# Delta rule: the off-diagonal blocks of the inverses in one group of matmuls a head, the first head's half of them amid its first gate projection

## The chip, the cores and the metric

The kernel runs on one core of one Trainium2 chip. The metric is the device time of one execution in microseconds (us), the median of several runs. Beside the timed runs there is one execution under the hardware profiler; all rows of the profile come from it, and times inside it are counted from the start of its span.

## The reference

The reference is one layer of a hybrid decoder for a prompt of 1024 tokens with 16 learned tokens ahead of it and a sample group of 8 sequences of 8 tokens: a half-step feed-forward network, a mixer, and a second half-step network. The mixer projects the tokens once and runs two branches, a gated delta rule with 8 heads and a sliding-window attention. What matters here is the delta rule for the prompt. In each chunk it solves a unit lower triangular system (cut):

```python
a_mat = jnp.where(strict, beta[..., :, None] * kk * decay, 0.0) + jnp.eye(c, dtype=q.dtype)
sol = lax.linalg.triangular_solve(a_mat, rhs, left_side=True, lower=True, unit_diagonal=True)
...
u = u_b - jnp.einsum('nhcd,nhde->nhce', w_c, s)
o = jnp.einsum('nhcd,nhde->nhce', qd_c, s) + jnp.einsum('nhij,nhje->nhie', qk_c, u)
s = s * cd_c[..., None, None] + jnp.einsum('nhcd,nhce->nhde', kd_c, u)
```

The reference uses chunks of 64 tokens. The kernel uses chunks of 128, eight a head, and holds the transposed inverse of each chunk's matrix as a tile of 128 x 128. Such an inverse has two diagonal blocks of 64 x 64, the inverses of the halves, and one off-diagonal block, the product of one half's inverse, the block of the matrix between the halves, and the other half's inverse.

## The kernel before, in words

The kernel goes through the layer in stages: first network, keys of all heads, window attention, the heads of the delta rule, output projection, second network. The change is in the stage of the heads (`heads`, L1664), between 1272 and about 1837 us of the profiled execution.

TensorE's order is written by hand: `body` puts it under a manual schedule (L1889), so TensorE executes matmuls exactly in the order in which the program's text issues them. The order of every other engine, and of the loads on the sync queue (SP), is set by a planner, which simulates the program while it is built; single instructions can be pinned to the order of the text. Waits between engines follow from the tiles that an instruction reads and writes. A tile with one buffer cannot be filled again before its last reader is done.

Streams of work are generators, and `weave` (L145) interleaves them. Each stream has a start, an end and a number of steps; step i of n stands at start + (end - start) (i + 0.5) / n, and the steps of all streams are issued in the order of these positions.

For each head h the streams are:

- `chain(h)`, 29 steps: the recurrence over the sample and eight chunks. Chunk t multiplies by the inverse in L1615, `R[:, i, :]` of the tile for t // 4.
- `qv_steps` and `z_gate`: projections, long runs of matmuls into the tile "gu" (L128, L130, L132), three for each of 8 slices of the model's width, in pieces of 512, 256 and 320 or 336 columns. They fill TensorE between the steps of the others.
- `prep8(h)`: three steps of preparation for the sample group (L1503 for "kq", L1541, L1550); its loads are "kq", "dt8" and "kd8".
- `prep(h, g)`: preparation of four chunks, g = 0 for chunks 0 to 3 and g = 1 for chunks 4 to 7. It has five steps, and each takes a turn of the PSUM tile "tr", one bank with one buffer: the off-diagonal first products (L1466, copied to "xt" by ScalarE in L1468), the values' transposes (L1474, scaled by ScalarE in L1476), the off-diagonal second products (L1480, copied into R in L1482), the squares of the queries (L1503, L1505), and keys by queries (L1491, finished by VectorE in L1493). Its first step also issues all loads of the group: the diagonal blocks into R (two, L1454), the transposed inverses "rt" (L1455), the matrix blocks "bo" (L1456), then kf, pm and kd; and GpSimd clears the lower left block of R (L1451).

The first and second products are matmuls of 64 x 64 at tile positions (0, 64) and (64, 0) of the array: the first reads partitions 0 to 63 and writes 64 to 127, the second the other way.

`prep(h, 1)` runs in the first 35% of head h. `prep8(h + 1)` and `prep(h + 1, 0)` run as `early(h + 1)`, eight steps, in the last quarter of head h (the last fifth of head 0). For head 0 there is a separate beginning, `early0` (L1669): its eight steps stand in the last 30% of the first 72 matmuls of head 0's gate projection z0. Its order is the off-diagonal first products, one step of `prep8`, nine small loads of the sample's inverses (`solves8`, "r8", L1430 and L1431), the other four steps of `prep`, and the last two of `prep8`.

Of the kernel before, what the change touches and what calls it, by code (L numbers as in the profile page):

```python
# [18 lines left out]
P = 128  # L19
# [120 lines left out]
def drain(steps):  # L140
    for _ in steps:
        pass


def weave(*streams):  # L145

    order = sorted((a + (b - a) * (i + 0.5) / n, j) for j, (g, a, b, n) in enumerate(streams) for i in range(n))
    for _, j in order:
        next(streams[j][0], None)
    for g, *_ in streams:  # L150
        drain(g)
# [7 lines left out]
def steps_of(g, n):  # L159

    return itertools.islice(g, n)
# [493 lines left out]
H = 8  # L655
# [43 lines left out]
class Mixer:  # L699
# [733 lines left out]
    def persistent(self, pool):  # L1433
        c, nc = self.c, self.nc
        self.ms = [c.t(pool, [P, 8, P], tag=f"ms{i}") for i in range(1)]
        self.p8 = [c.t(pool, [80, P], tag=f"p8{i}") for i in range(2)]
        self.on8 = c.t(pool, [P, 1, P], tag="on8")
        for m in (*self.ms, *self.p8, self.on8):
            nc.gpsimd.memset(m, 0.0)

    def prep(self, h, g, pool):

        c, nc = self.c, self.nc
        T = lambda shape, tag, bufs=None, dt=F32: c.t(pool, shape, dt, tag=tag, bufs=bufs)
        x = self.hd[h]
        ts = range(4 * g, 4 * g + 4)
        cols = slice(4 * g * P, (4 * g + 4) * P)
        R = x["R", g] = T([P, 4, P], f"R{g}")
        rt = T([64, 4, 64], "rt", 2)
        bo = T([64, 4, 64], "bo", 2)  # L1450
        nc.gpsimd.memset(R[64:P, :, 0:64], 0.0)  # L1451
        for half in range(2):
            r = slice(half * 64, half * 64 + 64)
            nc.sync.dma_start(R[r, :, r], self.lr_d[h, ts.start:ts.stop, half].rearrange("t r c -> r t c"))  # L1454
        nc.sync.dma_start(rt, self.lrt_d[h, ts.start:ts.stop, 0].rearrange("t r c -> r t c"))  # L1455
        nc.sync.dma_start(bo, self.bo_d[h][:, ts.start:ts.stop])  # L1456
        kf = x["kf", g] = T([P, 4, P], f"kf{g}")
        nc.sync.dma_start(kf, self.kf_d[h][:, cols].rearrange("p (t k) -> p t k", k=P))
        pm = x["pm", g] = T([P, 4, P], f"pm{g}")
        nc.sync.dma_start(pm, self.dt_d[h][:, ts.start:ts.stop, :])  # L1460
        kd = x["kd", g] = T([P, 4, P], f"kd{g}")
        nc.sync.dma_start(kd, self.kd_d[h][:, ts.start:ts.stop, :])

        px = self.ps([P, 4, P], "tr")
        for t in range(4):
            nc.tensor.matmul(px[64:P, t, 0:64], bo[:, t, :], rt[:, t, :], start=True, stop=True, tile_position=(0, 64))  # L1466
        xt = T([P, 4, 64], "xt")
        nc.scalar.copy(xt[64:P], px[64:P, :, 0:64])  # L1468
        yield

        vs = x["vs", g] = T([P, 4, P], f"vs{g}")
        pt = self.ps([P, 4, P], "tr")
        for i, t in enumerate(ts):
            nc.tensor.transpose(pt[:, i, :], x["cv"][:, t * P:(t + 1) * P], self.k(C_IDENT))  # L1474
        for i, t in enumerate(ts):
            nc.scalar.activation(vs[:, i, :], pt[:, i, :], AF.Copy, scale=self.nr[:, h, t:t + 1])  # L1476
        yield
        px = self.ps([P, 4, P], "tr")
        for t in range(4):
            nc.tensor.matmul(px[0:64, t, 0:64], xt[64:P, t, :], R[64:P, t, 64:P], start=True, stop=True,  # L1480
                             tile_position=(64, 0))
        nc.scalar.copy(R[0:64, :, 64:P], px[0:64, :, 0:64])  # L1482
        yield

        cq = x["cq", g] = T([P, 4], f"cq{g}")
        self.squares(h, cq, [x["qv"][:, t * P:(t + 1) * P] for t in ts], pool)
        yield

        pk = self.ps([P, 4, P], "tr")
        for i, t in enumerate(ts):  # L1490
            nc.tensor.matmul(pk[:, i, :], kf[:, i, :], x["qv"][:, t * P:(t + 1) * P], start=True, stop=True)  # L1491
        for i, t in enumerate(ts):
            nc.vector.scalar_tensor_tensor(out=pm[:, i, :], in0=pk[:, i, :], scalar=self.s[:, h, t:t + 1],  # L1493
                                           in1=pm[:, i, :], op0=ALU.mult, op1=ALU.mult)
        yield
# [58 lines left out]
    def chain(self, h, pool):  # L1554
# [44 lines left out]
        for t in range(8):  # L1599
            if t % 4 == 0:  # L1600
                on = T([P, 4, P], "on", 3)
                vs, kf, R, kd, pm = (x[k, t // 4] for k in ("vs", "kf", "R", "kd", "pm"))
            i = t % 4
# [10 lines left out]
            px = self.ps([P, P], "ch", 2)  # L1614
            nc.tensor.matmul(px, R[:, i, :], b, start=True, stop=True)  # L1615
            xs = T([P, P], "xs", 2)
# [47 lines left out]
    def heads(self, pool, mg):  # L1664
        def early(h):
            yield from self.prep8(h, pool)
            yield from self.prep(h, 0, pool)

        def early0():  # L1669
            prep = self.prep(0, 0, pool)  # L1670
            yield from steps_of(prep, 1)
            yield from steps_of(prep8, 1)
            self.solves8(pool)
            yield from prep
            yield from prep8

        z0 = self.z_gate(0, pool)
        prep8 = self.prep8(0, pool)
        weave((steps_of(z0, 72), 0, 1, 72), (early0(), 0.7, 1, 8))
        for h in range(H):  # L1680
            streams = [(self.chain(h, pool), 0, 1, 29), (self.prep(h, 1, pool), 0, 0.35, 5)]
            if h:
                streams += [(self.emit(h - 1, pool), 0, 0.2, 3)]
            if h < H - 1:
                if h:
                    streams += [(self.qv_steps(h + 1, pool), 0, 0.5, 145), (self.z_gate(h, pool), 0.5, 1, 145)]
                else:
                    streams += [(self.qv_steps(1, pool), 0, 0.55, 145), (z0, 0.55, 1, 73)]
                streams += [(early(h + 1), 0.75 if h else 0.8, 1, 8)]
            else:  # L1690
                out = self.emit(h, pool)
                streams += [(self.z_gate(H - 1, pool, mg.load_w), 0, 0.95, 145), (steps_of(out, 2), 0.6, 1.15, 2)]
                begin = mg.begin()
                streams += [(steps_of(begin, 1), 0.6, 0.6, 1)]
            weave(*streams)
        weave((begin, 0, 1, 42), (out, 0.1, 0.2, 1), (self.left, 0.15, 0.5, 4))
        drain(mg.begin_last(self.hd[H - 1]["Z"][:, 0:P]))
# [496 lines left out]
```

## Time and profile before

| what | us |
|---|---|
| median of 3 runs | 2669.71 |
| lowest and highest run | 2668.64 and 2669.86 |
| the profiled execution's own time | 2674.25 |
| span of the profiled execution | 2672.4 |
| mean granted TensorE clock over the span | 0.99 |

In the rows, PE is TensorE's matmuls and PEld its weight loads, DVE is VectorE, ACT is ScalarE, POOL is GpSimd, SPq is the sync queue that issues loads. A row names the line, the engine, the operation, the tile written and the tiles read, the shape and the count. A matmul in full precision has two records. In a time-ordered row the first two numbers are the start and the length of the row's instructions taken together, and the brackets at the end say how long the engine sat idle before and who ended that. In a row of waits the three numbers are the total in us, the number of times, and the longest.

### The profile page before, as it was taken

Reading aid. Unit: us, or ns where it says so; the run is one execution under the profiler, and the core shown is the slowest. Engines: PE = TensorE matmul, PEld = TensorE weight load, DVE = VectorE, ACT = ScalarE, POOL = GpSimd, SP = SyncE. Lnnn points to the kernel's source line nnn. Section 1 sums busy time; section 2 is a strip of 40 time slices with the busy share of each in tenths; the row PEclk is TensorE's granted clock in tenths of the full one; section 3 lists DMA queues with packets and bytes.
Section 4 is the critical chain, followed back from the end, with each engine's and each line's share of the span. In section 5 each row is a group of like instructions: output and inputs, shape, how many; then the busy total and the mean of one; then the engine's idle time right before and its main releaser. Section 6 shows DMA issues by size and latency. Waiting matters only on the chain. (4 is left out here: it accounts for less than half of the span.)

```text
span 2672.4 us, 49500 instructions
## 1 busy us (share of the span) xinstructions
PE 2606.7 (98%) x19053; PEld 2486.6 (93%) x19053; DVE 1552.0 (58%) x2315; ACT 1127.5 (42%) x2718; POOL 1270.3 (48%) x1205
## 2 busy tenths in 40 slices
PE   7999999999999999999999999999999999999998
PEld 7999999999988998888889999997789999999998
DVE  7657565546677726995444444444556656654566
ACT  6333343422146734457444444454533434334221
POOL 6656555445525533433334333335555555554471
PEclk9999999999999999999999999999999999999999
DMA  4344343667545744345332233334433433338764
GB/s 165 122 150 155 122 167 117 248 230 250 190 141 165 222 140 130 114 135 158 102 99 89 87 97 96 100 93 159 163 107 139 164 128 149 127 138 318 241 226 142
DMA packets 229570, 406.47 MB, mean 152 GB/s; under 512 B 59751, under 2 KB 121351, under 8 KB 229047
## 3 DMA queue, kind: packets, MB, share of 16 engines
q1 hardware_dynamic: 209030, 324.75, 37.5%
q10 hardware_dynamic: 20304, 78.56, 7.4%
q8 instruction: 150, 2.46, 0.4%
q14 instruction: 86, 0.70, 0.1%
HBM read 264.36 MB, written 140.53 MB: 152 GB/s over the span
## 5 line engine op out<-in xcount | busy, mean ns | idle before, releaser
L132 PE MATMUL gu<-xh,wl 128*128 128x512 f32 (+3 forms) x1456 | 496.5, 341 | 0.0
L128 PE MATMUL gu<-xh,wh 128*128 128x512 f32 (+3 forms) x1456 | 492.3, 338 | 0.0
L130 PE MATMUL gu<-xl,wh 128*128 128x512 f32 (+3 forms) x1456 | 490.9, 337 | 0.0
L282 POOL TENSOR_TENSOR wl<-T,wh 128x512 fp32r<-128x512 f32 x246 | 331.2, 1353 | 319.2 <-ACT wh L281 251.7
L496 PE MATMUL y<-hb,wh 128*128 128x256 f32 (+2 forms) x2528 | 430.3, 290 | 3.3 <-DVE acc L507 1.8
L282 POOL TENSOR_TENSOR wl<-raw,wh 128x512 fp32r<-128x512 f32 x200 | 283.1, 1424 | 252.2 <-ACT wh L281 189.4
L496 PEld LDWEIGHTS y<-hb,wh 128*128 128x128 f32 x2528 | 365.9, 188 | 4.4 <-DVE acc L507 2.2
L281 ACT CAST wh<-T 128x512 fp32r<-128x512 f32 x246 | 152.5, 621 | 363.4 <-PE B L316 111.4
L132 PEld LDWEIGHTS gu<-xh,wl 128*128 128x128 f32 x1456 | 277.4, 191 | 16.6 <-issue 0.4
L128 PEld LDWEIGHTS gu<-xh,wh 128*128 128x128 f32 x1456 | 277.3, 190 | 16.7 <-issue 0.9
L130 PEld LDWEIGHTS gu<-xl,wh 128*128 128x128 f32 x1456 | 277.2, 190 | 16.6 <-issue 0.4
L496 PE MATMUL y<-hb,wl 128*128 128x256 f32 (+2 forms) x1264 | 271.6, 288 | 0.0
L281 ACT CAST wh<-raw 128x512 fp32r<-128x512 f32 x200 | 122.4, 621 | 279.4 <-PE C L316 82.9
L770 POOL TENSOR_TENSOR wl<-raw,wh 128x1024 fp32r<-128x1024 f32 x58 | 141.0, 2430 | 180.9 <-ACT wh L769 173.5
L507 DVE TENSOR_TENSOR acc<-acc,y 128x552 f32<-128x552 f32 (+4 forms) x216 | 144.7, 679 | 138.1 <-PE y L496 137.8
L496 PEld LDWEIGHTS y<-hb,wl 128*128 128x128 f32 x1264 | 206.9, 188 | 0.0
L256 DVE TENSOR_TENSOR T<-raw,raw 128x512 f32<-128x512 f32 x124 | 118.6, 961 | 108.0 <-POOL wl L282 108.0
L1570 POOL TENSOR_TENSOR f<-f,mhalf 128x1 f32<-128x1 f32 (+1 forms) x72 | 54.8, 761 | 126.2 <-DVE f L1568 124.6
L267 DVE TENSOR_TENSOR T<-raw,T 128x512 f32<-128x512 f32 x62 | 65.6, 1061 | 61.9 <-POOL wl L282 61.8
L256 DVE TENSOR_TENSOR T<-raw,T 128x512 f32<-128x512 f32 x62 | 62.1, 1010 | 32.0 <-POOL wl L282 31.6
L1075 DVE TENSOR_TENSOR ltmp<-la 72x14 f32<-72x14 f32 (+37 forms) x76 | 71.9, 946 | 12.6 <-DMA la<-b_d 11.6
L769 ACT CAST wh<-raw 128x1024 fp32r<-128x1024 f32 x60 | 63.0, 1050 | 38.1 <-PE gu L130 38.1
(593 smaller groups left out, 7312.5 us busy)
## 6 DMA issues: line engine op xcount, KB each, us to landing
hb<-hid SPq DMA_DIRECT2D x71, 552.0 KB
hb<-hid SPq DMA_DIRECT2D x71, 544.0 KB
hid<-hs ACTq DMA_DIRECT2D x69, 552.0 KB
hid<-hs ACTq DMA_DIRECT2D x69, 544.0 KB
raw<-in_w_in_dram SPq DMA_DIRECT2D x58, 512.0 KB
raw<-in_ffn_w_gate_dram SPq DMA_DIRECT2D x100, 256.0 KB
raw<-in_ffn_w_up_dram SPq DMA_DIRECT2D x94, 256.0 KB
raw<-in_ffn_w_down_dram SPq DMA_DIRECT2D x88, 256.0 KB
```

What stands on the lines that cost most here:

```text
L128: nc.tensor.matmul(ps, wh, xh, start=first and i == 0, stop=False)
L130: nc.tensor.matmul(ps, wh, xl, start=False, stop=False)
L132: nc.tensor.matmul(ps, wl, xh, start=False, stop=last and i == n - 1)
L256: pin(self.nc.vector.tensor_tensor(out=b[name], in0=b[x], in1=b[y], op=ALU.subtract))
L267: nc.vector.tensor_tensor(out=s, in0=b["21"], in1=s, op=ALU.subtract)
L281: self.nc.scalar.copy(hi, s)
L282: self.nc.gpsimd.tensor_tensor(out=lo, in0=s, in1=f32(hi), op=ALU.subtract)
L496: self.nc.tensor.matmul(self.view(ps[d], (i,)), w[x][:, d * P:(d + 1) * P], hb[:, y, lo:hi], start=j + x + y == 0, stop=j == len(items) - ...
L507: dve = lambda out, x, y: nc.vector.tensor_tensor(out=out, in0=x, in1=y, op=ALU.add)
L769: nc.scalar.copy(hi, raw)
L770: low.tensor_tensor(out=lo, in0=raw, in1=f32(hi), op=ALU.subtract)
L1075: pin(nc.vector.tensor_tensor(out=t, in0=a[:n, 0:j, j:j + 1].to_broadcast([n, j, w]), in1=a[:n, j:j + 1, j + 1:size].to_broadcast([n, j, w ...
```

## The change

The off-diagonal blocks of both halves of a head are made in one step, and the first products are made one head ahead:

- `persistent` allocates three tiles R and clears them once. Group 0 of every head uses R[0]; group 1 uses R[1] or R[2] in turn.
- `inverses(h)` issues the four loads of diagonal blocks for the whole head. `off_load(h)` loads "rt" and "bo" for all eight chunks of a head, one buffer each.
- The first step of `prep(h, 0)` now issues eight second products for head h and, in the same bank, eight first products for head h + 1; then come one copy of 64 x 512 to "xt" and two copies of 64 x 256 into R. The two off-diagonal steps of `prep` are gone, so `prep(h, 0)` has four steps and `prep(h, 1)` three.
- For head 0, `off0` makes the eight first products in one step at 0.45 of the first 72 matmuls of z0. `early0` begins with the step of `prep8` and the nine "r8" loads and has seven steps.

The diff, with the unchanged lines around it cut:

```diff
@@ persistent
+        self.R = [c.t(pool, [P, 4, P], tag=f"R{i}") for i in range(3)]
+        self.xt = {}
-        for m in (*self.ms, *self.p8, self.on8):
+        for m in (*self.ms, *self.p8, self.on8, *self.R):
             nc.gpsimd.memset(m, 0.0)
+    def inverses(self, h, pool):
+        x, nc = self.hd[h], self.nc
+        for g in range(2):
+            R = x["R", g] = self.R[g + g * (h % 2)]
+            for half in range(2):
+                r = slice(half * 64, half * 64 + 64)
+                nc.sync.dma_start(R[r, :, r], self.lr_d[h, 4 * g:4 * g + 4, half].rearrange("t r c -> r t c"))
+        if 0 < h < H - 1:
+            self.off_load(h + 1, pool)
+    def off_load(self, h, pool):
+        rt, bo = (self.c.t(pool, [64, 8, 64], tag=tag) for tag in ("rt", "bo"))
+        self.nc.sync.dma_start(rt, self.lrt_d[h, :, 0].rearrange("t r c -> r t c"))
+        self.nc.sync.dma_start(bo, self.bo_d[h])
+        self.off = rt, bo
+    def first_products(self, h, px, pool):
+        rt, bo = self.off
+        for t in range(8):
+            self.nc.tensor.matmul(px[64:P, t], bo[:, t], rt[:, t], start=True, stop=True, tile_position=(0, 64))
+        self.xt[h] = self.c.t(pool, [P, 8, 64], tag="xt")
+        self.nc.scalar.copy(self.xt[h][64:P], px[64:P])
+    def second_products(self, h, px):
+        xt = self.xt.pop(h)
+        for t in range(8):
+            self.nc.tensor.matmul(px[0:64, t], xt[64:P, t], self.hd[h]["R", t // 4][64:P, t % 4, 64:P], start=True,
+                                  stop=True, tile_position=(64, 0))
+    def blocks_out(self, h, px):
+        for g in range(2):
+            self.nc.scalar.copy(self.hd[h]["R", g][0:64, :, 64:P], px[0:64, 4 * g:4 * g + 4])
@@ prep(h, g)
-        R = x["R", g] = T([P, 4, P], f"R{g}")
-        rt = T([64, 4, 64], "rt", 2)
-        bo = T([64, 4, 64], "bo", 2)
-        nc.gpsimd.memset(R[64:P, :, 0:64], 0.0)
-        for half in range(2):
-            r = slice(half * 64, half * 64 + 64)
-            nc.sync.dma_start(R[r, :, r], self.lr_d[h, ts.start:ts.stop, half].rearrange("t r c -> r t c"))
-        nc.sync.dma_start(rt, self.lrt_d[h, ts.start:ts.stop, 0].rearrange("t r c -> r t c"))
-        nc.sync.dma_start(bo, self.bo_d[h][:, ts.start:ts.stop])
+        if not g:
+            self.inverses(h, pool)
...
-        px = self.ps([P, 4, P], "tr")
-        for t in range(4):
-            nc.tensor.matmul(px[64:P, t, 0:64], bo[:, t, :], rt[:, t, :], start=True, stop=True, tile_position=(0, 64))
-        xt = T([P, 4, 64], "xt")
-        nc.scalar.copy(xt[64:P], px[64:P, :, 0:64])
-        yield
+        if not g:
+            px = self.ps([P, 8, 64], "tr")
+            self.second_products(h, px)
+            if h < H - 1:
+                self.first_products(h + 1, px, pool)
+            self.blocks_out(h, px)
+            yield
...
-        yield
-        px = self.ps([P, 4, P], "tr")
-        for t in range(4):
-            nc.tensor.matmul(px[0:64, t, 0:64], xt[64:P, t, :], R[64:P, t, 64:P], start=True, stop=True,
-                             tile_position=(64, 0))
-        nc.scalar.copy(R[0:64, :, 64:P], px[0:64, :, 0:64])
@@ heads
+        def off0():
+            self.first_products(0, self.ps([P, 8, 64], "tr"), pool)
+            self.off_load(1, pool)
+            yield
         def early0():
             prep = self.prep(0, 0, pool)
-            yield from steps_of(prep, 1)
             yield from steps_of(prep8, 1)
...
+        self.off_load(0, pool)
-        weave((steps_of(z0, 72), 0, 1, 72), (early0(), 0.7, 1, 8))
+        weave((steps_of(z0, 72), 0, 1, 72), (off0(), 0.4, 0.5, 1), (early0(), 0.7, 1, 7))
-            streams = [(self.chain(h, pool), 0, 1, 29), (self.prep(h, 1, pool), 0, 0.35, 5)]
+            streams = [(self.chain(h, pool), 0, 1, 29), (self.prep(h, 1, pool), 0, 0.35, 3)]
...
-                streams += [(early(h + 1), 0.75 if h else 0.8, 1, 8)]
+                streams += [(early(h + 1), 0.75 if h else 0.8, 1, 7)]
```

## Prediction

> **What bounds the kernel now.** I read the page first, for the engine that fills the span.
>
> ```profile
> PE 2606.7 (98%) x19053; PEld 2486.6 (93%) x19053; DVE 1552.0 (58%) x2315; ACT 1127.5 (42%) x2718; POOL 1270.3 (48%) x1205
> ```
>
> TensorE is busy for 98% of the span. Since the diff touches only the stage of the heads, I then cut that stage into stretches: the first gate projection with the first early step, head 0, and heads 1 to 6.
>
> ```profile
> core 0: us, PE busy (x) PEld busy (x) DVE busy (x) ACT busy (x) POOL busy (x), PEclk, DMA share, GB/s
> 1272.00:1296.00 24.00, 20.87 (x128) 17.73 (x127) 9.28 (x15) 10.00 (x31) 8.88 (x19) 0.93 0.59 160
> 1296.00:1360.00 64.00, 61.31 (x409) 55.47 (x407) 29.09 (x58) 30.53 (x105) 19.76 (x31) 0.95 0.28 78
> 1360.00:1775.00 415.00, 415.00 (x2873) 381.29 (x2873) 185.34 (x393) 196.90 (x657) 158.86 (x199) 1.00 0.32 94
> ```
>
> From 1360 to 1775 us TensorE is busy for all 415 us at the full clock: it waits for nothing there, and only TensorE time itself can be saved. The first stretch is another case: 3.1 us idle, and a granted clock of 0.93, which costs 24 x 0.07 = 1.7 us more. Head 0 loses 64 x 0.05 = 3.2 us to the clock. The view of the tile "tr" says what TensorE stood for in the first stretch (each row ends in the starts of the first and the last matmul):
>
> ```profile
> L1466 PE MATMUL tr<-rt,bo x8: 218/218/267, 1281.2 to 1281.7; 64*64 64x64 f32 x8
> L1480 PE MATMUL tr<-R,xt x8: 218/218/267, 1285.1 to 1285.6; 64*64 64x64 f32 x8
> L1491 PE MATMUL tr<-qv,kf x8: 275/275/377, 1288.6 to 1289.5; 128*128 128x128 f32 x8
> L1474 PE MATMUL tr<-ident,cv x4: 272/273/327, 1283.2 to 1283.6; 128*128 128x128 f32 x4
> L1503 PE MATMUL tr<-ident,qv x4: 272/272/308, 1286.3 to 1286.7; 128*128 128x128 f32 x4
> L1541 PE MATMUL tr<-kq x2: 423/448/473, 1291.0 to 1291.3; 128*128 128x64 f32 x2
> L1503 PE MATMUL tr<-ident,kq x1: 299/299/299, 1282.4 to 1282.4; 128*128 128x128 f32 x1
> its engine sat idle before it (us, times) until:
>   ACT sqp L1505: 1.4, 1
>   ACT vs L1476: 0.9, 1
>   DVE pm L1493: 0.8, 1
> ```
>
> All three waits, 3.1 us together, are for turns of the one "tr" bank: a group of matmuls cannot start before ScalarE or VectorE has emptied the bank of the group before. So the change meets two limits: TensorE's own time in the heads, and the chain of "tr" turns in the first stretch.
>
> **What one off-diagonal group costs.** Over the whole run both lines have 128 records, two to a matmul, so 64 matmuls, 16 groups of four for each line, 32 groups in all:
>
> ```profile
> L1466 PE MATMUL tr<-rt,bo x128: 218/218/366, 1281.2 to 1779.0; 64*64 64x64 f32 x128
> L1480 PE MATMUL tr<-R,xt x128: 218/218/367, 1285.1 to 1786.1; 64*64 64x64 f32 x128
> ```
>
> I looked at one group in the full stretch, in the order of time:
>
> ```profile
> 1485.81 0.28 PE L128 MATMUL gu<-xh,wh 128*128 128x256 f32 x1
> 1485.93 0.28 PE L130 MATMUL gu<-xl,wh 128*128 128x256 f32 x1
> 1486.14 0.68 PE L1466 MATMUL tr<-rt,bo 64*64 64x64 f32 x8
> 1486.75 0.39 PE L132 MATMUL gu<-xh,wl 128*128 128x256 f32 x1
> 1486.97 0.28 PE L128 MATMUL gu<-xh,wh 128*128 128x256 f32 x1
> ```
>
> and at the end of the same group alone:
>
> ```profile
> 1486.42 0.39 PE L1466 MATMUL tr<-rt,bo 64*64 64x64 f32 x4
> ```
>
> Projection matmuls of 256 columns start 0.12 us apart (1485.81 to 1485.93). From 1485.93 to 1486.97 are 1.04 us; two projection matmuls explain 0.24. The group's last four records, 0.39 us from first start to last end with 0.218 for the last, start (0.39 - 0.218) / 3 = 0.057 us apart, so eight explain 0.46. What is left, 1.04 - 0.24 - 0.46 = 0.34 us, is the price of entering and leaving the 64x64 position once, however many matmuls are in the group. One old group is 0.46 + 0.34 = 0.80 us.
>
> **The change part by part.**
>
> *Groups.* The number of matmuls stays. Before they stand in 32 groups, after in 9: one of first products in the gate projection, seven of second products together with the next head's first, and one of second products alone for head 7. 23 x 0.34 = 7.8 us of TensorE time go. 22 of the 23 lie where TensorE is the limit or nearly so (the two groups of the second half of heads 0 to 7, and one in each of six early steps); the last one is in head 0's early step.
>
> *The border* inside the seven joint groups, from position (64, 0) to (0, 64), is in no row of before. At the least it costs nothing. At the most I take that the first matmul waits until the last one is out: 0.218 - 0.057 = 0.16 us, 7 x 0.16 = 1.1 us. I take the gap that a group shows between its first four records and its last four (0.68 - 0.39 - 4 x 0.057 = 0.06 us more than the spacing), since that too is a start without the pipeline filled: 7 x 0.06 = 0.4 us.
> The Trainium skill ("TensorEngine Tiling (Array Packing)", Restrictions and Gotchas) speaks against the joint group: row tiles may not use one PSUM bank at the same time, and here both halves write one bank. By that rule the border would cost the far end, 1.1 us; no run here shows it yet.
>
> *The first stretch.* Two rows of ScalarE price the copies of the joint turn:
>
> ```profile
> 1277.90 0.60 ACT L1394 ACTIVATE tz<-gu 128x512 f32<-128x512 f32 x1 [6.43 <-PE gu L132]
> ...
> 1281.97 0.37 ACT L1468 COPY xt<-tr 64x256 f32<-64x256 f32 x1 [0.86 <-PE tr L1466]
> ```
>
> Today the turns of "tr", from start to start in the tile's rows, are: values 1283.2 to 1285.1 (1.9 us), second products to 1286.3 (1.2), squares to 1288.6 (2.3), keys by queries to 1291.0 (2.4); 7.8 us. After, the first products have their turn earlier, amid the gate projection, which hides their copy. That moves the sample's squares hardly at all: TensorE reaches them at 1281.2 + 0.34 + 16 x 0.057 = 1282.45, today 1282.4. But the joint turn is long: from its first matmul to the first copy 0.77 us today (1281.2 to 1281.97), with 24 records more 0.77 + 24 x 0.057 = 2.1; then three copies, of 512 columns and twice 256, 0.60 + 2 x 0.37 = 1.3. 3.5 + 1.9 + 2.3 + 2.4 = 10.1 us, so the last turn ends 2.3 us later. Of that, (0.34 + 0.91) + (0.34 + 1.82) - 2 x 0.80 = 1.8 us are TensorE work that moved in, which the count of groups has already. The stall grows by 2.3 - 1.8 = 0.5 us. Its bounds: -0.9 (the wait before the second products goes and nothing takes its place) and +3.9 (below).
>
> *Heads 1 to 6.* The joint turn's copies, 1.3 us, must be over before the values' transposes, which come 0.25 / 7 of a head later, 2.5 us of 70. Today the turn of squares takes 2.3 us in steps of 0.25 / 8, 2.2 us, and TensorE waits for none of them in its 415 us. I take 0; the far end is the smallest wait of the first stretch, 0.8 us, in six heads: 4.8 us.
>
> *With no cost:* 16 clearings of R on GpSimd go and three larger ones come; 16 load issues of the sync queue go; ScalarE has 0.60 + 2 x 0.37 instead of 4 x 0.37 us a head. All of it lies beside TensorE's full 415 us; without that cover it would be a saving. Only in the first stretch does their order count (rivals).
>
> **Sum:** -7.8 + 0.4 + 0.5 = -6.9 us. The profiled execution took 2674.25 us, 2672.4 of them span; it would take 2667.4. The median of the runs, 2669.71, is 4.5 lower, and I take the same 6.9 off it: **2662.8 us**, 0.26% less. About 0.2%, 5.3 us, is what a measurement of this kernel tells from no change.
>
> **The rivals.** Most of them live in the first stretch, on the sync queue:
>
> ```profile
> 1273.69 1.35 SPq L1454 DMA_DIRECT2D R<-lr_d  x2
> 1275.09 0.61 SPq L1455 DMA_DIRECT2D rt<-lrt_d  x1
> ...
> 1279.66 2.72 SPq L1430 DMA_DIRECT2D r<-l_d  x8
> ```
>
> and on GpSimd, which clears what they fill:
>
> ```profile
> 1273.68 0.98 POOL L1439 MEMSET ms<- 128x1024 f32 x1
> ...
> 1275.15 0.31 POOL L1451 MEMSET R<- 64x256 f32 x1
> 1275.52 1.20 POOL L940 COPY kq<-qv 128x64 f32<-128x64 f32 x1
> 1276.66 0.63 POOL L1427 MEMSET r<- 80x640 f32 x1
> ```
>
> *R's loads come late (0.16).* In the program's text the sample's nine loads "r" now stand ahead of R's four. "r" is cleared by 1277.3 today, then behind three clearings of 0.5 (half of 0.98) in place of one of 0.3: 1278.5. The nine take 9 x 2.72 / 8 = 3.1 us, R's four 4 x 0.67, so R is issued by 1284.3. What a load takes from issue I bound by what GpSimd waits for loads of yw:
>
> ```profile
> POOL Z L1660 <- DMA yw<-yw_d: 22.5, 8, 3.5
> ```
>
> 22.5 / 8 = 2.8 us: R lands at 1287.1, where TensorE wants it at 1283.2, 3.9 us. -6.9 + 3.9 = -3.0: 2666.7. For it: today's loads go in the text's order here. Against: R's own clearing ends over 1 us before that of "r".
>
> *The border drains (0.08).* -6.9 - 0.4 + 1.1 = -6.2: 2663.5; it is still faster.
>
> *One more fall of the clock (0.10).* The first stretch's clock fell to 0.93 though its idle waits were 1.4, 0.9 and 0.8 us; with a longer stall it could fall a second time, 1.7 us. -6.9 + 1.7 = -5.2: 2664.5.
> The Trainium skill ("TensorE: Matmul & The Clock Gate", Part 1: The HAM clock gate) lets the clock fall after an idle window of about 3.4 us; by that no wait here would do it. The row speaks otherwise: three shorter waits close together go with 0.93.
>
> *Joining saves nothing (0.07).* If the 0.34 us belonged to the matmuls and not to the group, only the stall's 0.5 us would remain: 2670.2. Against: records inside a group start 0.057 us apart.
>
> *Slower: the sync queue stands (0.12).* rt and bo have one buffer now, so head 1's load waits until TensorE has done head 0's first products, 20 projection matmuls earlier than today's 1281.2, 2.5 us at 0.12 or a little more: over at 1280.0. If it is queued directly behind head 0's, all that follows stands until then. Eight issues from rt's to r's took 1279.66 - 1275.09 = 4.57 us, 0.57 each: the pair and the sample's three loads end at 1282.8, "r" at 1285.9, R at 1288.6, landed at 1291.4 against 1283.2: 8.2 us, and two falls of the clock, 3.4. -6.9 + 11.6 = +4.7: 2674.4. It is slower once stall and clock together pass 6.9 us. For it, two rows of the queue's own waits in the first stretch:
>
> ```profile
> SPq L1514 <- PE tr L1541: 4.3, 1, 4.3
> SPq L1455 <- PE tr L1466: 1.6, 1, 1.6
> ```
>
> Against it, the row of rt's loads:
>
> ```profile
> L1455 SPq DMA_DIRECT2D rt<-lrt_d x16: 579/586/614, 1275.1 to 1711.0; - x16
> ```
>
> The queue does stand for TensorE, once 4.3 us, and 1.6 for just this buffer; but rt's last load is issued at 1711.0 and last used at 1779.0, so such pairs are sent well ahead of their turn, not in the text's order.
>
> **How the numbers follow.** The forecast has 0.47; with the border, 0.55 is faster by over 0.2%. The clock, R's loads, no saving and 0.05 of the standing queue are within: 0.38. The rest of that rival, if yet more loads land late, is slower: 0.07. The range goes from the forecast without the falls of the clock that stand there now, 1.7 us and half of head 0's 3.2 (2659.5), to R's loads with the border and one more fall (2666.7 + 0.7 + 1.7 = 2669.1); it leaves out the last two rivals, 0.19.
>
> **What would show it.** Nine groups of 64x64, each 0.34 us by the same working; heads 1 to 5 shorter by 3 x 0.34 = 1.0 us each at the full clock without idle TensorE. In the first stretch a wait before the values' transposes in place of the one before the second products; R or rt as a releaser means a queue rival. The forecast is wrong if the joint groups have a gap of 0.3 us at the border, or if TensorE is idle in heads 1 to 6.

## The result and the profile after

The changed kernel is slower. Its median is 2676.71 us over 12 runs (2669.80 to 2679.58), against 2669.78 over 12 runs of the kernel before on the same chip (2666.76 to 2673.41). The ratio is 1.0026 with a 95% interval from 1.0019 to 1.0034, so 5 to 9 us more, where the prediction had 6.9 less and a range that ended at 2669.1. The profiled execution took 2677.80 us, 2675.9 of them span, at a mean granted clock of 0.989 (before 2674.25, 2672.4 and 0.990).

The first part of the page gives the busy times:

```profile
PE 2598.9 (97%) x19053; PEld 2483.0 (93%) x19053; DVE 1547.6 (58%) x2315; ACT 1124.0 (42%) x2710; POOL 1261.3 (47%) x1192
```

TensorE is busy for 7.8 us less than before, with the same number of matmuls, and the span is 3.5 us longer all the same. TensorE must stand still somewhere. The view by windows, cut at the ends of the first gate projection and of head 0, says where:

```profile
core 0: us, PE busy (x) PEld busy (x) DVE busy (x) ACT busy (x) POOL busy (x), PEclk, DMA share, GB/s
1275.90:1308.00 32.10, 26.01 (x147) 22.26 (x147) 9.00 (x15) 11.06 (x33) 6.57 (x20) 0.73 0.51 133
1308.00:1368.50 60.50, 57.01 (x404) 51.97 (x403) 26.68 (x58) 30.22 (x104) 20.46 (x28) 1.00 0.29 81
1368.50:1778.00 409.50, 404.82 (x2843) 375.50 (x2842) 186.84 (x390) 191.66 (x639) 155.28 (x188) 1.00 0.32 94
```

The same cut of the kernel before:

```profile
1272.20:1294.70 22.50, 19.37 (x115) 16.23 (x115) 9.16 (x15) 10.00 (x31) 7.38 (x19) 0.92 0.60 164
1294.70:1358.30 63.60, 60.91 (x404) 55.06 (x403) 27.50 (x58) 30.53 (x105) 19.45 (x30) 0.95 0.28 80
```

The first stretch is 9.6 us longer, and its granted clock is 0.73 instead of 0.92: by that 32.1 x 0.27 = 8.7 us go to the clock, against 22.5 x 0.08 = 1.8. Both are upper bounds, since TensorE also stood still for part of the time at half clock. Head 0 is 3.1 us shorter, about the 63.6 x 0.05 = 3.2 us that the clock took there before; its three groups fewer (1.0 us) and 0.8 us more of waiting nearly cancel. In the later heads TensorE, which had stood for nothing, is idle for 409.50 - 404.82 = 4.7 us. Heads 1 to 6 take 3.0 us less together, half of the 1.0 each that the groups should save, and head 7 0.75 less. So the stage is 9.6 - 3.1 - 3.0 - 0.75 = 2.7 us longer in this pair of profiles; the rest of the pair's 3.5 lies outside the stage.

Two waits stand behind this. In the first stretch, the view of the tile "tr" and the waits:

```profile
L1464 PE MATMUL tr<-rt,bo x32: 217/288/364, 1282.5 to 1294.1; 64*64 64x64 f32 x32
L1471 PE MATMUL tr<-R,xt x16: 310/311/362, 1290.7 to 1292.7; 64*64 64x64 f32 x16
```

```profile
PE tr L1471 <- DMA R<-lr_d: 4.0, 2, 3.8
```

The first products have their turn at 1282.5, amid the projection, but the joint group begins only at 1290.7: TensorE waits 3.8 us, and then 0.2, for R's loads. The sync queue in order of time shows why they were late:

```profile
1277.41 0.67 SPq L1457 DMA_DIRECT2D rt<-lrt_d  x1
...
1280.68 0.60 SPq L1451 DMA_DIRECT2D R<-lr_d  x1
1283.64 0.59 SPq L1457 DMA_DIRECT2D rt<-lrt_d  x1
1284.33 0.58 SPq L1458 DMA_DIRECT2D bo<-bo_d  x1
1284.97 2.91 SPq L1430 DMA_DIRECT2D r<-l_d  x8
1287.92 0.31 SPq L1431 DMA_DIRECT2D r<-l_d  x1
1288.28 1.90 SPq L1451 DMA_DIRECT2D R<-lr_d  x3
```

and the queue's own waits have the reason for its gap:

```profile
SPq L1457 <- PE tr L1464: 2.0, 1, 2.0
```

One of R's four loads is issued at 1280.68. Then the queue stands until 1283.64, since head 1's rt needs the buffer that head 0's first products still read. After that come bo, all nine loads of "r", and only then R's other three, the second of the four at 1288.28 and the last at 1289.56. TensorE's two starts, at 1290.65 and 1291.95 on its timeline, come 2.4 us behind these two issues. That fits the program: the first four second products read the block that the second load brings, the other four that of the last. Both of the prediction's queue rivals happened, one behind the other.

The clock in steps of 2 us (three consecutive rows, and later ones):

```profile
1286.00:1288.00 2.00, 0.83 (x6) 0.56 (x5) 0.58 (x2) 0.49 (x3) 0.00 (x0) 1.00 0.26 52
1288.00:1290.00 2.00, 0.00 (x0) 0.00 (x0) 0.00 (x0) 0.00 (x0) 0.00 (x0) 1.00 0.22 37
1290.00:1292.00 2.00, 1.13 (x9) 0.97 (x9) 0.00 (x0) 0.00 (x0) 0.00 (x0) 0.56 0.56 110
...
1300.00:1302.00 2.00, 1.09 (x6) 1.04 (x6) 0.17 (x1) 1.94 (x11) 0.00 (x0) 0.50 0.26 49
...
1306.00:1308.00 2.00, 2.00 (x9) 1.67 (x8) 0.21 (x1) 1.65 (x3) 0.49 (x1) 0.67 0.12 24
```

TensorE ran dry at about 1286.83 (0.83 us into the first row). The clock falls to one half at about 1290.2, some 3.4 us later, and comes back only at about 1307.3: 17.1 us at half speed. In between the turns of "tr" make TensorE wait 0.3 to 0.9 us four times, the last wait ending at 1304.3.

The second wait is in the heads. The waits from 1360 to 1780 us:

```profile
PE tr L1471 <- ACT vs L1575: 3.6, 6, 0.6
PE ch L1639 <- DVE b L1631: 1.0, 1, 1.0
```

Six times TensorE stands for 0.6 us before the joint group, until ScalarE has emptied "tr" of the sample's values (L1575). The cause of the one wait of 1.0 us for VectorE, in head 3, is open; it is 0.5 us in the second profile of this kernel, 0.2 to 0.5 in five of the edited kernels, and absent before. ScalarE in order of time at the end of head 1:

```profile
1423.88 0.60 ACT L1394 ACTIVATE tz<-gu 128x512 f32<-128x512 f32 x1 [0.90 <-PE gu L132]
1424.38 1.56 ACT L1548 ACTIVATE kds<-kd,smask 80x128 f32<-80x128 f32 x5
1425.84 0.35 ACT L1575 ACTIVATE vs<-tr,nr__1447_9701 80x128 f32<-80x128 f32 x1
```

The copy itself takes 0.35 us. Ahead of it stand a copy of the gate (0.60), for which ScalarE first sat idle for 0.90 us, and the five masked copies of the sample's keys (1.56), which the same step of `prep8` issues. The transposed values could have been copied well before that: their matmul starts at 1423.86 and takes 0.27 us. The same place in the kernel before, on ScalarE and then on TensorE:

```profile
1414.30 1.56 ACT L1524 ACTIVATE kds<-kd,smask 80x128 f32<-80x128 f32 x5
1415.77 0.35 ACT L1551 ACTIVATE vs<-tr,nr__1447_9701 80x128 f32<-80x128 f32 x1
1416.02 0.58 ACT L1394 ACTIVATE tz<-gu 128x512 f32<-128x512 f32 x1
```

```profile
1416.37 0.68 PE L1466 MATMUL tr<-rt,bo 64*64 64x64 f32 x8
```

There the gate's copy came behind the values' copy, which was over at 1416.12, 0.25 us before TensorE wanted the bank. With seven early steps in the last quarter in place of eight the step falls elsewhere in the gate projection; the gate's copy now stands first, and the margin of 0.25 us becomes a wait of 0.6. That the number of steps decides the order is a reading, but with eight steps again ("A step between", below) the gate's copy does stand behind the values' copy.

The joint group itself, on TensorE's timeline after such a wait:

```profile
1425.37 0.28 PE L128 MATMUL gu<-xh,wh 128*128 128x256 f32 x1
1426.24 0.97 PE L1471 MATMUL tr<-R,xt 64*64 64x64 f32 x13 [0.60 <-ACT vs L1575]
1427.00 0.27 PE L1464 MATMUL tr<-rt,bo 64*64 64x64 f32 x1
1427.05 0.22 PE L1471 MATMUL tr<-R,xt 64*64 64x64 f32 x1
...
1427.22 0.92 PE L1464 MATMUL tr<-rt,bo 64*64 64x64 f32 x13
1428.07 0.39 PE L130 MATMUL gu<-xl,wh 128*128 128x256 f32 x1
```

At the border records of the two positions alternate 0.05 us apart. There is no gap there at all.

### The profile page after: what moved, and what is told of

It reads as the page before. It is cut to its first block, busy times and chain, and to the rows that moved or that the text cites. A ratio compares the mean times of both kernels' runs of the same rounds, so it can differ in the third digit from the quotient of the medians.

```text
span 2675.9 us, 49432 instructions
## 1 busy us (share of the span) xinstructions
PE 2598.9 (97%) x19053; PEld 2483.0 (93%) x19053; DVE 1547.6 (58%) x2315; ACT 1124.0 (42%) x2710; POOL 1261.3 (47%) x1192
## 5 line engine op out<-in xcount | busy, mean ns | idle before, releaser
L130 PEld LDWEIGHTS gu<-xl,wh 128*128 128x128 f32 x1456 | 277.8, 191 | 17.1 <-issue 0.7
L930 DVE SCALAR_TENSOR_TENSOR cv<-pc,cw,cv 128x1131 f32<-128x1131 f32 x48 | 66.8, 1393 | 21.4 <-POOL cv L927 20.8
```

Of the source, the lines that this page charges most:

```text
L130: nc.tensor.matmul(ps, wh, xl, start=False, stop=False)
L930: nc.vector.scalar_tensor_tensor(out=cv, in0=pc[:, w:w + PADW], scalar=self.cw[:, j, w:w + 1], in1=cv, op0=ALU.mult, op1=ALU.add)
```

## The experiments

Three theories were set against each other. **A**: R's late loads in the first stretch, with the clock that they cost. **B**: the six waits for ScalarE. **C**: neither matters much, and the difference is how the clock happens to fall in one program and not in another. All kernels are the changed kernel with the edit shown, compared with the kernel before on the same chip: 34 runs with a median of 2668.59 us for the first four, 24 runs with 2669.74 for the others. Since the kernels do the same work otherwise, their ratios can be set beside each other.

**R's loads first.** Head 0's loads of R are issued before the projection, directly behind rt and bo.

```diff
@@ prep(h, g)
-        if not g:
+        if not g and h:
             self.inverses(h, pool)
@@ heads
         self.off_load(0, pool)
+        self.inverses(0, pool)
```

> Edit: the four loads of head 0's diagonal blocks into R are issued right behind the loads of rt and bo, ahead of the first gate projection; nothing else differs from the changed kernel. Theory A (late blocks): the changed kernel loses in the first stretch, where the second products wait 3.8 us for R's load and the clock then stays at half for 17 us; here the wait for R is gone, the stretch from the first gate matmul to head 0's first matmul falls from 32.1 us to under 27, and the median falls by 5 to 9 us, to 2668 to 2672. Theory B (ScalarE's turns in heads 1 to 6 eat the saving): the six waits of 0.6 us before the joint groups stay, and the median falls by no more than the 3.8 us of the wait itself. Theory C (the loss lies outside the stage, in where the clock falls): the median stays within 2 us of 2676.7 though the wait is gone.

Measured: 2667.39 us (11 runs), ratio 0.9991 (0.9982 to 0.9999). The wait for R is gone, and the waits of the first stretch are those for turns of "tr" that were there in kind before:

```profile
PE tr L1515 <- ACT sqp L1529: 1.3, 1, 1.3
PE tr L1527 <- ACT vs L1506: 0.8, 1, 0.8
PE tr L1504 <- ACT R L1476: 0.7, 1, 0.7
```

The stretch takes 25.7 us at a granted clock of 0.87, 6.4 less than in the profile of the changed kernel. The six waits in the heads remain, 3.6 us. From 1.0026 to 0.9991 are 0.35%, 9.3 us, with some 3 us to each side from the two intervals: the 4.0 us of idle TensorE cost about twice their length. A is borne out, and it alone turns the slowdown into about no change.

**A step between.** The early work of a head waits one step between `prep8` and `prep`, so that projection matmuls lie between the values' copy and the joint group.

```diff
@@ early(h)
             yield from self.prep8(h, pool)
+            yield
             yield from self.prep(h, 0, pool)
...
-                streams += [(early(h + 1), 0.75 if h else 0.8, 1, 7)]
+                streams += [(early(h + 1), 0.75 if h else 0.8, 1, 8)]
```

> Edit: from head 1 on an empty step stands between the sample's preparation and the joint group (eight steps in place of seven), so the joint group comes 4.4 us behind the sample's values in place of 2.5; nothing else differs from the changed kernel. Theory B: the six waits of 0.6 us for ScalarE's copy of the sample's values are gone, heads 1 to 6 are 0.7 us shorter each, and the median falls by about 4.5 us to 2672. Theory A: the first stretch is as before, with its 3.8 us wait and the low clock, so the kernel stays slower than the kernel before, by 2 us or more. A rival to B: the waits only move to the next turn of the bank (the values or the squares), and the median stays at 2676 to 2677.

Measured: 2671.35 us (12 runs), ratio 1.0002 (0.9992 to 1.0012). The six waits are gone. The head from the first sample matmul of head 2 to that of head 3 takes 68.51 us, against 69.18 in the changed kernel and 69.76 before. The wait for R stays, 4.0 us, and the first stretch takes 29.9 us at 0.83. From 1.0026 to 1.0002 are 0.24%, 6.4 us, more than the 6 x 0.67 = 4.0 us of the rows, but the intervals, some 2.5 us to each side, leave that open. B is borne out too.

**The sample's loads later.** `early0` begins with the joint group's step, so that R's loads come ahead of the nine loads of "r" in the text, while head 1's rt stays where it is. This splits the wait for R into its two causes.

```diff
@@ early0
             yield from steps_of(prep8, 1)
+            yield from steps_of(prep, 1)
             self.solves8(pool)
```

> Edit: in the first early step the nine loads of the sample's inverses are put behind the loads of R, kf, pm and kd in the text; nothing else differs from the changed kernel. Two parts of theory A are told apart. If the nine loads ahead of R's last three make the wait (3.2 us of issue time), the wait of the second products falls from 3.8 us to under 1.5 and the median by 4 us or more. If the queue's standing for rt's buffer makes it (2.4 us without an issue), R's last three loads still come behind that, and a wait of 1.5 us or more stays. Theories B and C: as for the first edit.

Measured: 2671.41 us (12 runs), ratio 1.0008 (0.9999 to 1.0016). The wait for R shrinks but does not go:

```profile
PE tr L1471 <- DMA R<-lr_d: 1.2, 2, 0.6
```

Of 4.0 us, 2.8 came from the nine loads ahead of R and 1.2 are left to the queue that stands for rt's buffer. The clock of the stretch is still 0.76. A second buffer for rt and bo, which would take the standing away by itself, was not tried.

**Both together.** The first two edits in one kernel.

> Both edits: R's loads of head 0 first, and the empty step from head 1 on. If A and B are both right they add up: no wait for R, no six waits of 0.6 us, TensorE idle under 2 us in heads 1 to 6, and a median of 2662 to 2667, below the kernel before, near what was forecast for the change. If only A is right: as the first edit alone, within 2 us. Theory C: within 2 us of 2676.7.

Measured: 2663.78 us (10 runs), ratio 0.9977 (0.9968 to 0.9986): 0.23% or 6 us less than before. The windows of the first stretch and of the heads:

```profile
1274.00:1299.70 25.70, 22.44 (x146) 19.17 (x146) 9.28 (x15) 11.07 (x33) 7.11 (x20) 0.87 0.58 163
1360.00:1770.00 410.00, 409.74 (x2883) 380.29 (x2882) 188.37 (x399) 196.57 (x652) 157.38 (x189) 1.00 0.33 95
```

In the heads TensorE is idle for 0.26 us of 410, and a head takes 68.5 us. With A and B both gone the change gives about what the prediction's sum had, 6.9 us; within the interval, some 2.5 us to each side, they account for what went wrong.

**Two groups in place of a joint one.** On top of that kernel, the first products of the next head stand one step behind the second products, in the joint groups of heads 1 to 6, which are made at the ends of heads 0 to 5. It gives up the joining and keeps all else.

```diff
@@ prep(h, g)
             self.second_products(h, px)
+            if h:
+                yield
             if h < H - 1:
                 self.first_products(h + 1, px, pool)
```

> Starting from the kernel with both edits (R's loads of head 0 first, the empty step). Edit: from head 1 on, the second products and the next head's first products stand in two steps, with projection matmuls between them, in one turn of the bank; the matmuls and the copies are the same. If the price belongs to the group (0.34 us for each entry into the 64x64 position), heads 1 to 5 get longer by 0.34 us each, from 68.5 to 68.9 us, without a new wait. If it belongs to the matmuls, or if what the joint group saves is a turn of the bank, they stay at 68.5. The median moves by 2 us, at the edge of what can be measured; the heads' lengths in the trace decide.

Measured: 2667.70 us (10 runs), ratio 0.9994 (0.9985 to 1.0003). Head 2 takes 69.27 us in place of 68.52, and each of heads 1 to 5 takes 0.75 to 0.92 us more, over twice the 0.34 expected, without a new wait of note; head 6, at whose end no joint group is made, takes 0.21 more. The single group of first products on TensorE's timeline:

```profile
1420.04 0.28 PE L132 MATMUL gu<-xh,wl 128*128 128x256 f32 x1
1420.25 1.14 PE L1464 MATMUL tr<-rt,bo 64*64 64x64 f32 x16
1421.33 0.39 PE L128 MATMUL gu<-xh,wh 128*128 128x256 f32 x1
1421.55 0.28 PE L130 MATMUL gu<-xl,wh 128*128 128x256 f32 x1
```

From 1420.04 to 1421.55 are 1.51 us; two projection matmuls explain 0.24 and sixteen records 16 x 0.057 = 0.91. What is left is 0.36 us, for sixteen records, as it was 0.34 for eight. So the price belongs to the group, not to the matmuls, and the rival that joining saves nothing is out. Entry (0.36) and the lost overlap at the border (0.14, worked out below) make 0.50 of the 0.75 us; where the other 0.25 goes is open.

**Values first.** R's loads first, as above, and the steps of the heads left where the change put them. Only ScalarE's order is changed: the five masked copies are issued behind the values' copy.

```diff
@@ prep8(h), third step
-        masked(range(4, 9))
         vs = x["vs8"] = T([P, P], "vs8")
...
         nc.scalar.activation(vs[:80], pt[:80, 0, :], AF.Copy, scale=self.nr[:80, h, 8:9])
+        masked(range(4, 9))
```

> Starting from the kernel with R's loads of head 0 first and without the empty step. Edit: ScalarE's copy of the sample's values out of the bank stands ahead of the five masked copies of kd in its order, in place of behind them. If those five copies (1.6 us) hold the bank, the six waits of 0.6 us before the joint groups are gone though the steps stand where the change put them, heads 1 to 5 fall from 69.2 to about 68.5 us, and the median falls by about 4 us against the one edit, to 2663 to 2664. If the joint group's place 2.5 us behind the values is too early in itself, the waits stay.

Measured: 2663.12 us (6 runs), ratio 0.9973 (0.9961 to 0.9985), the same as with the step between. All six waits are gone. ScalarE in order of time:

```profile
1413.13 0.35 ACT L1574 ACTIVATE vs<-tr,nr__1447_9701 80x128 f32<-80x128 f32 x1
1413.38 1.57 ACT L1548 ACTIVATE kds<-kd,smask 80x128 f32<-80x128 f32 x5
```

The gate's copy (0.60 us) still stands ahead of the values' copy here, and the joint group comes at the same place. So that place is not too early in itself: without the masked copies ahead of the values' copy TensorE does not wait. The step between takes the same waits away by moving the joint group and the gate's copy.

**The first stretch spread out.** On top of both edits, the first products of head 0 and its early steps are moved forward in the projection, so that more projection matmuls lie between two turns of "tr".

```diff
-        weave((steps_of(z0, 72), 0, 1, 72), (off0(), 0.4, 0.5, 1), (early0(), 0.7, 1, 7))
+        weave((steps_of(z0, 72), 0, 1, 72), (off0(), 0.25, 0.35, 1), (early0(), 0.5, 1, 7))
```

> Starting from the kernel with both edits. Edit: head 0's first products stand at 0.3 of the 72 gate matmuls in place of 0.45, and the seven early steps from 0.5 on in place of 0.7. If the chain of turns of the bank bounds the first stretch, more gate matmuls cover its waits: the four waits there (0.7, 0.8, 1.3 and 0.4 us) fall by half or more, the stretch falls from 25.7 to 21 to 23.5 us, the clock falls less, and the median goes 2 to 4 us below that of both edits, to 2660 to 2662. Rival: rt's second load and R's loads come too late for the earlier steps and a wait for DMA takes the place of the four; then the stretch stays at 25 us or more.

Measured: 2661.10 us (7 runs, 2659.04 to 2663.69), ratio 0.9968 (0.9957 to 0.9979). This is the fastest of all, 0.32% or 8.5 us below the kernel before. The window of the first stretch:

```profile
1270.70:1293.60 22.90, 19.54 (x147) 16.69 (x147) 8.78 (x14) 10.85 (x33) 6.02 (x19) 1.00 0.68 183
```

It is 2.8 us shorter than with both edits alone, but 25.7 x 0.13 = 3.3 us of that other stretch went to the clock, which stays at 1.00 here. Beside a stretch at the same clock (23.3 us, in the last section) it is 0.4 us shorter. The waits did not halve: 1.0, 0.6, 0.5 and 0.5 us for turns of "tr", and a new one of 0.8 for the load of bo, which now has less time. The gain over the kernel with both edits, 0.09%, is within the two intervals.

**The changed kernel again**, without an edit, as the test of C.

> The changed kernel itself once more, to have it on the same chip as the others. The wait of 3.8 us for R, the six of 0.6 us and heads of 69.2 us should be there again; how long the clock stays at half in the first stretch, and so the time, may differ by some us. Theory C (luck of the clock) would have it within 2 us of the kernel before this time.

Measured: 2676.28 us (11 runs), ratio 1.0021 (1.0012 to 1.0031); the waits are the same, 4.0 us for R and six of 0.6. So the slowdown repeats, and C falls as an explanation of the median. It holds for single runs: this kernel's profiled execution took 2670.35 us, 7.5 less than the first one, and its first stretch was at half clock for a shorter time:

```profile
1271.20:1301.10 29.90, 23.42 (x146) 19.78 (x146) 8.79 (x14) 10.66 (x33) 6.02 (x19) 0.83 0.55 142
```

A granted clock of 0.83 costs at most 29.9 x 0.17 = 5.1 us, against 8.7 in the other profile of the same kernel.

**What the clock cost over all runs.** Each run lists its mean granted clock to three decimals. The mean over runs is 0.992 for the kernel before (0.9918), and 0.9915 to 0.9921 for the five kernels without the wait for R; for the kernels that have it, it is 0.9888 and 0.9889 (the changed one), 0.9894 (the step between) and 0.990 (the short wait). The changed kernel loses (0.9918 - 0.9888) x 2670 = 8 us more to the clock, at the most, since the mean also counts time in which TensorE stood still. Only kernels that wait for R have the lower clock, so the wait is shown to be its cause. Which of these 8 us fall in the first stretch and which elsewhere no single profile says: in the pair of profiles the stretch accounts for at most 8.7 - 1.8 = 6.9, and head 0 gives back 3.2. Counted by TensorE's busy time the stretch's share is less: 26.01 - 19.37 = 6.6 us more, and without the 1.8 that the prediction reckoned as work moved in, 4.8.

## Why the prediction was wrong, point by point

**The group's price: right.** "23 x 0.34 = 7.8 us of TensorE time go": TensorE's busy time fell by 7.8 us, in part by chance, since busy time also holds the slower matmuls at half clock. The cleaner proof is the head without waits: 68.52 us instead of 69.76, 1.24 less, for three groups (3 x 0.34 = 1.02) and the border. One slip of the count changes no number: the last of the 23 groups is saved in head 7's early step, not in head 0's, which has two groups before and after.

**The border: wrong in sign, small.** "I take the gap that a group shows": +0.06 us for each joint group. In the kernel with both edits, from the last projection matmul before the joint group to the second one after it are 1419.96 - 1417.70 = 2.26 us, as these rows show:

```profile
1417.70 0.28 PE L130 MATMUL gu<-xl,wh 128*128 128x256 f32 x1
1417.91 0.97 PE L1471 MATMUL tr<-R,xt 64*64 64x64 f32 x13
...
1419.73 0.39 PE L132 MATMUL gu<-xh,wl 128*128 128x256 f32 x1
1419.96 0.28 PE L128 MATMUL gu<-xh,wh 128*128 128x256 f32 x1
```

Two projection matmuls take 0.24, 32 records 32 x 0.057 = 1.82; only 0.20 is left for entry and border, 0.14 less than one entry. In the joint group shown with the result the records alternate at the border: matmuls of the second position start before the last ones of the first, which fits an overlap there. The bound was "at the least it costs nothing", without a reason that excluded a gain. The rule of the Trainium skill that the prediction weighed ("TensorEngine Tiling (Array Packing)", Restrictions and Gotchas, no one PSUM bank for two row tiles at the same time) would have made it dearer; the rows show both halves written in one bank 0.05 us apart, at no cost in time.

**The first stretch: the step that failed.** "The stall grows by 2.3 - 1.8 = 0.5 us." It priced the turns of "tr" and took for granted that the joint group finds its operands. The turns were priced about right: in the profile of the values-first kernel the stretch has no half clock and takes 23.3 us, where the prediction's 2.3 on top of today's stretch without the clock's share gives 22.5 - 1.8 + 2.3 = 23.0. But R came 3.8 us late. The rival "R's loads come late" had 3.9 us, right in size by luck, from two errors that cancel: it left out the standing queue (2.4 us), and it let TensorE start 2.8 us behind the last of R's four issues, where TensorE started 2.4 us behind the second (1288.28 to 1290.65), 0.5 us after the last issue was over, and lost only 0.2 us more to the last load. "Such pairs are sent well ahead of their turn" was no argument against the standing queue: rt was sent ahead, and being ahead was why it stood for its buffer. Both rivals rest on the same thing, a queue that issues in order with other loads ahead of R's, so their chances should not have been shared out as if one excluded the other.

**The clock: mis-sized.** "With a longer stall it could fall a second time, 1.7 us." That is one fall of 3.4 us at half clock. In every profile of this case the granted clock changes only in steps of 3.41 us, and a fall lasts one or several of them: one in the first stretch of the kernel before and two in its head 0 (6.8 us), but five (17.1 us) in one profile of the changed kernel and three (10.2 us) in the other. With the wait for R the clock took 5 to 8 us more: 4.8 by TensorE's busy time in the pair of profiles, at most 8 by the mean clock over the runs. The forecast treated a fall as an event with a fixed price. What ends a fall is not shown. In the second profile of the changed kernel the clock came back 1.7 us behind a wait of 0.4 us, with waits of 1.0 and 0.8 us still ahead, and in head 0 of the kernel before it stayed at half for 6.8 us in which TensorE was busy throughout. The Trainium skill ("TensorE: Matmul & The Clock Gate", Part 1: The HAM clock gate) has the clock fall after some 3.4 us idle and rise after about as much sustained work. The steps of 3.41 us fit that length, but not the idle time: the clock fell 3.4 us after TensorE ran dry in the first profile of the changed kernel, 2.7 us after in the second and 2.8 in that of the step between; and the falls in kernels whose longest wait is 1.3 us do not follow from the idle half of the rule. The same page of the Trainium skill, in its section "A second HAM failure mode: psum-queue depth-cycling", names such a case, short idle times between groups of matmuls, without a price.

**Heads 1 to 6: the other step that failed.** "TensorE waits for none of them in its 415 us. I take 0." The comparison was of lengths: a turn of 2.3 us fitted into steps of 2.2 us. The joint group does not follow such a turn. It looked at what comes behind the joint group, not at what comes ahead of it: the sample's values, whose copy stands behind 2.2 us of other work on ScalarE (0.60 + 1.56), and whose margin before was only 0.25 us. The far end of that term, 6 x 0.8 = 4.8 us, held what came, 6 x 0.67 = 4.0 us, but by luck, since it was taken from another wait. The condition that the prediction named as its own refutation, idle TensorE in heads 1 to 6, is what the profile showed.

**The whole.** With 4.0 us of waits in the heads, 4.0 for R and 5 to 8 of clock, the forecast's -6.9 becomes +6 to +9; measured were 5 to 9. Without the first two, and so without the third, the kernel is 0.23% faster (0.14 to 0.32), where 0.26% was forecast.

## What to carry to other kernels

When a step moves on a saturated engine, look up two queues for it: the loads that it needs, with every load that the in-order queue holds ahead of them (one waiting for a single buffer holds all that follow), and the engine that must empty its bank, with all that stands ahead of the emptying copy. A wait that lets the clock fall costs more than its length, and how much more differs from run to run: here taking away 4 us of idle gave about 9, with some 3 to each side. The switch from 128x128 to 64x64 and back is paid once a group, 0.34 us here, so joining groups pays as long as the joined group finds its bank and its loads.

## What the runs showed of the hardware that was not expected

- Matmuls at tile positions (64, 0) and (0, 64) that write the two halves of one PSUM bank alternate at the border, record by record, 0.05 us apart, which fits an overlap: the joint group is 0.14 us cheaper than 32 records and one entry.
- The granted clock changed only in steps of 3.41 us, in all ten profiles. One wait of 3.8 us left it at half for 17.1 us in one execution and 10.2 in another of the same kernel; two waits of 0.6 us with the short turns behind them still gave 13.7 us, 0.76 over 28 us.
- The same kind of waits went with a granted clock of 0.87 in the kernel with R's loads first (1.3, 0.8 and 0.7 us, above) and with 1.00 in the values-first kernel (1.3, 0.8, 0.8 and 0.7 us), whose first stretch is this window:

```profile
1274.90:1298.20 23.30, 19.66 (x146) 16.64 (x146) 8.78 (x14) 9.21 (x30) 6.02 (x19) 1.00 0.65 175
```

So the lengths of such waits alone do not settle whether the clock falls. Where they lie in the steps of 3.41 us may: with R's loads first one step holds 1.9 us of the waits of 0.8 and 1.3 us, TensorE is busy for 0.46 of it, and the clock falls at its end; in the values-first kernel no step holds more than 1.6 us, the emptiest is busy for 0.53, and the clock stays. No threshold follows from this: in other profiles the clock fell behind a step that was busy for 0.66 (the short wait for R) and stayed behind one of 0.52 (the changed kernel again). Single executions of one kernel differ for it: the runs of the changed kernel go from 2669.80 us at a mean clock of 0.992 to 2679.58 at 0.988.
